# A state-space layer that starts from the unscaled sum, with 1/rms applied to its products and its decays masked by GpSimd

## The chip, the cores and the metric

The kernel runs on one core of a Trainium2 chip. The metric is the device time of one execution in microseconds (us). Below, PE is TensorE, DVE is VectorE, ACT is ScalarE, POOL is GpSimd and SP is the engine that issues most DMAs.

## The reference, cut to what matters

Two blocks run one after the other on 256 tokens of width 1024. The first ends with a mixture of 32 experts, whose weighted outputs are added to the stream. The second begins with a state-space layer that reads the normed stream:

```python
x = x + hier_moe(hn, ...)                      # x2 in the kernel
# second block, layer 0
u = x * rsqrt(mean(x*x) + EPS) * w             # rms_norm
proj = u @ in_w                                # z | x, B, C | dt
xbc = silu(conv4(proj[x, B, C]) + conv_b)      # 4 taps along the tokens, per channel
dt = softplus(proj[dt] + dt_bias);  a = dt * -exp(a_log)
a_cum = cumsum(a in chunks of 128 tokens)
decay_in = exp(where(causal, a_cum[t] - a_cum[s], -inf))     # per head, 32 heads
y = (C B^T * decay_in) x dt + state terms + D x
y = group_rms_norm(y * silu(z)) @ out_w
```

Afterwards come a second layer (latent attention) and a last norm, which the change doesn't touch.

## The kernel before, in words

Everything is in one program whose engines work through queues fixed when it is built; semaphores tie them together. Matmuls of weights at high accuracy are made of three products: a weight chunk `raw` is split into a high part by ACT (`W`, the cast in L101) and a low part by DVE (the subtraction in L101), both in a tile `whl`. Four to six such tiles exist.

Experts run in 8 groups of 4. For group q, `gate_up(q)` and `down(q)` multiply 32 rows by streamed weights; the side work `ex_side(q)` scatters the outputs of the group before back to the tokens (`scatter`: four products of the one-hot matrix `ST` with `ysb`, 128x512 each, L1096, added to `x2_sb` on DVE, L1097). After group 7's `down` its own scatter follows, each of its parts with a sum of squares on ACT (L352), then the check on whether an expert got more tokens than its rows hold (`overflow`, an If that all engines pass, L1663), then 1/rms (`rstd_of`).

The state-space layer turns `x2` with the diagonal `dr` of 1/rms (`norm_T`, 32 products of 128x128, L376). These pieces, times the gain, become `uh` and `ul` (ACT L379, DVE L380), the layer's input with features on partitions. Nine products into `acc` stand ahead of it (L1162). The units of the layer follow in this order: z0 (`gemm_first`, L411 to L413, 48 products of 512 columns, tokens on partitions), dt (24 small ones), then B0, B1, C0, C1, x0, x1, z1, x2, z2, x3, z3 (`fine_feat` and `fine_tok`, L417, 96 products of 256 columns or 48 of 512). Each fills one of two PSUM tiles `acc` of 128x1024. A queue of generators `Q` weaves other work between the products of a unit: `conv` on the unit just done, `decay(g)` for 8 groups of 4 heads, `silus`, `couple(g)` (C B^T times the decays `L`), `ssd(g)`, `gate` and so on.

`decay(g)` takes two heads at a time. Two products with the 64-row selector `id2` spread the cumulated decays over 128 partitions (L1233), 20 products of the unit later one product adds `negm`, minus 2 to the 100th where not causal (L1241), and ACT takes the exponentials, 128x128 each: two with bias `toend` (L1237), four with bias `ncum` (L1246). `conv` reads `acc` on ACT (four 128x256, L1255) and on DVE (twelve, L1260).

Of the kernel before, what the change touches and what calls it, by code (L numbers as in the profile page):

```python
# [18 lines left out]
P = 128  # L19
T = 256  # L20
# [10 lines left out]
WARM2 = 9  # L31
# [180 lines left out]
def model_kernel(ctx: ExitStack, tc: tile.TileContext, ap, out, taps=None, stop=None):  # L212
# [64 lines left out]
    def gain_row(pool, v):  # L277

        g = pool.tile([P, D], F32, name="gb", tag="gb")
        return g, nc.sync.dma_start(g, v.to_broadcast([P, D]))  # L280
# [104 lines left out]
    def gemm_first(xh, xl, norm, ps, steps):  # L385

        cs = {}
        for step in steps:  # L390
            if step is None:
                W.behind = ()
                continue
# [575 lines left out]
    with ExitStack() as b2:  # L969
# [105 lines left out]
        def down(q):  # L1075
            y = [yp.tile([P, 512], F32, name="yps") for _ in range(2)]
            h = hT.pop(q)
            for k in range(4):
                ws, used = W.whole(2)
                for half in range(2):  # L1080
                    for j in range(4):
                        nc.tensor.matmul(y[half][quad(j)], h[:, k, quad(j)], ws[j // 2][:, j % 2, HALF[half]],  # L1082
                                         start=(k == 0), stop=(k == 3))
                W.done(used)
            ys[q] = w2.tile([P, 1024], F32, name="ysb", bufs=1)
            for half in range(2):
                nc.scalar.copy(ys[q][:, HALF[half]], y[half])  # L1087

        def scatter(q, ST, done=None):

            y = ys.pop(q)
            for half in range(2):
                s = HALF[half]
                for t in range(2):
                    m = mp.tile([P, 512], F32, name="m")
                    nc.tensor.matmul(m, ST[:, t * P:(t + 1) * P], y[:, s], start=True, stop=True)  # L1096
                    nc.vector.tensor_add(x2_sb[:, t, s], (x2_sb if q else x_sb)[:, t, s], m)  # L1097
                    if done:
                        done(t, half)
                    yield  # L1100
# [13 lines left out]
        for q in range(8):  # L1114
            run_steps(gate_up(q), ex_side(q))
# [8 lines left out]
        idr = k2.tile([P, P], F32R, name="idr")  # L1124
        nc.vector.tensor_copy(idr, ident)
        id2 = k2.tile([64, 32], F32R, name="id2")
        nc.vector.tensor_add(id2, ident[:64, 0:32], ident[:64, 32:64])
        negm = k2.tile([P, P], F32R, name="negm")
        nc.vector.tensor_scalar(negm, G, -2.0 ** 100, None, op0=OP.mult)
# [3 lines left out]
        def x2_square(t, q):  # L1133
            square_sum(x2_sb[:, t, HALF[q]], junk, x2ss[:, t, q:q + 1])
# [16 lines left out]
    with ExitStack() as b3:  # L1151
# [11 lines left out]
        gemm_first(uh, ul, [norm_T(t, r2[t], R_N2, k3, mp, uh, ul) for t in range(2)], ps,  # L1163
                   ((None, 0), (None, 1), 0, 1, (None, 2), 0, 0, (None, 3), 0, 0, (0, 0), (0, 1), 1, 1, (0, 2), (0, 3),
                    1, 1, (1, 0), (1, 1), (1, 2), (1, 3)))
        zt = {0: w2.tile([P, 2, 512], F32, name="zs")}
        nc.scalar.activation(zt[0].rearrange("p a b -> p (a b)"), ps, AF.Silu)
# [3 lines left out]
        for k in range(8):  # L1171
            mm3(ps_d[:32, :T], h[:, k], l[:, k], uh[:, k], ul[:, k], k == 0, k == 7)
        nA = wk.tile([P, 32], F32, name="nA")
        xf = wk.tile([32, T], F32, name="xf")
        nc.scalar.activation(xf, ps_d[:32, :T], AF.Identity, bias=vec[:32, R_DTB:R_DTB + 1])
# [4 lines left out]
        chl = wk.tile([64, T], F32R, name="chl")  # L1180
# [26 lines left out]
        def sums():  # L1207
# [6 lines left out]
            nc.scalar.copy(chl, cum)  # L1214
# [12 lines left out]
        def decay(g):  # L1227

            for j in range(2):
                m = mp.tile([P, 2, T], F32, name="m")  # L1230
                for i in range(2):
                    h = 4 * g + 2 * j + i
                    nc.tensor.matmul(m[:, i], id2[:, h:h + 1].to_broadcast([64, P]), chl, start=(i == 0), stop=False,  # L1233
                                     skip_group_check=True)
                for i in range(2):
                    h = 4 * g + 2 * j + i
                    nc.scalar.activation(L[g][:, 1, 2 * j + i], m[:, i, P:], AF.Exp, bias=toend[:, h:h + 1])  # L1237
                for _ in range(10):
# [4 lines left out]
                for i in range(2):  # L1243
                    h = 4 * g + 2 * j + i
                    for c in range(2):
                        last["exp"] = nc.scalar.activation(L[g][:, 2 * c, 2 * j + i], m[:, i, c * P:(c + 1) * P],  # L1246
                                                           AF.Exp, bias=ncum[:, c, h:h + 1])
# [4 lines left out]
        def conv(ps, ct, f0):  # L1252
            for n in range(4):
                f = f0 + n
                nc.scalar.activation(ct[:, n], ps[:, n * T:(n + 1) * T], AF.Identity, bias=vcol(R_CB + f),  # L1255
                                     scale=convw[:, 3, f:f + 1])
            for k in range(2, -1, -1):
                d = 3 - k
                for n in range(4):
                    nc.vector.scalar_tensor_tensor(ct[:, n, d:], ps[:, n * T:(n + 1) * T - d],  # L1260
# [117 lines left out]
        for kind, u in (("x", 0), ("x", 1), ("z", 1), ("x", 2), ("z", 2), ("x", 3), ("z", 3)):  # L1378
# [7 lines left out]
            else:  # L1386
                Q.weave(fine_tok(uh, ul, ps), 48)
                zt[u] = w2.tile([P, 2, 512], F32, name="zs")
                z = nc.scalar.activation(zt[u].rearrange("p a b -> p (a b)"), ps, AF.Silu)  # L1389
# [30 lines left out]
    with ExitStack() as b4:  # L1420
# [6 lines left out]
        fw, dma = gain_row(k2, ap["final_norm_w_2"][None, :])  # L1427
# [230 lines left out]
def overflow(tc, nc, ap, raw, mp, yp, ep, ovi, wov, rx, g2, iof, ident, x_sb, x2_sb, after):  # L1658
# [4 lines left out]
    with tc.If(n > 0):  # L1663
        with ExitStack() as es:
            ov = es.enter_context(tc.tile_pool(name="ov", bufs=1))
            xf = raw.tile([P, 8, T], F32, name="raw", tag="raw")
            h4 = raw.tile([P, 4, 512], F32, name="raw", tag="raw")
# [11 lines left out]
            with tc.For_i(0, 32) as e:  # L1679
# [9 lines left out]
                def load(name, k0, n):  # L1689

                    wt = ov.tile([P, 1024], F32, name="owt")
# [6 lines left out]
                for name in ("w_expert_gate", "w_expert_up"):  # L1698
                    m = [ep.tile([P, 512], F32, name="ea") for _ in range(2)]
                    for k in range(8):  # L1700
                        if k % 2 == 0:
                            wt = load(name, k, 2)
                        for t in range(2):
                            nc.tensor.matmul(m[t], xf[:, k, t * P:(t + 1) * P], wt[:, k % 2], start=(k == 0),
# [6 lines left out]
                hT = ov.tile([P, 4, T], F32, name="ohT")  # L1711
# [5 lines left out]
                for half in range(2):  # L1717
                    s = slice(half * 512, half * 512 + 512)
                    y = [yp.tile([P, 512], F32, name="yps") for _ in range(2)]
                    for k in range(4):  # L1720
                        wt = load("w_expert_down", k, 1)
                        for t in range(2):
                            nc.tensor.matmul(y[t], hT[:, k, t * P:(t + 1) * P], wt[:, 0, s], start=(k == 0),
# [3 lines left out]
            for t in range(2):  # L1727
                for half in range(2):
                    after(t, half)
# [62 lines left out]
```

## Time and profile before

| | us |
|---|---|
| time, median of 3 runs (1091.69 to 1092.43) | 1092.33 |
| the profiled execution's own time | 1093.37 |
| its span | 1091.7 |
| mean granted TensorE clock in it | 0.992 |
| 240 to 635 us of the span | experts |
| 635 to 648.5 us | end of the experts to the state-space layer's first product |
| 648.5 to 877 us | state-space layer |

The profile was taken from one execution, 1.04 us longer than the median of the runs. Time in its rows is counted from the span's start. A stage is read by which engine is busy throughout, and by what an engine's idle time ended on.

### The profile page before, as it was taken

What the parts mean: (1) busy time and instruction counts of PE and PEld (TensorE: products, weight loads), DVE (VectorE), ACT (ScalarE), POOL (GpSimd) and SP (SyncE); (2) the same over time, 40 slices, a digit from 0 to 9 for tenths busy, and PEclk for the clock granted to TensorE, in tenths of its full rate; (3) what the DMA queues carried; (4) which work ended last, traced back from release to release, by engine and by line L of the source; (5) the groups of instructions that cost most, each with busy time, mean ns of one, the idle gap of its engine ahead of it and who ended that gap; (6) DMA issues with size and microseconds to landing.
All of it is one profiled execution on the core that took longest, in us unless ns stands there. A gap on an engine that the chain in (4) does not pass through costs nothing. (4 is left out here: it accounts for less than half of the span.)

```text
span 1091.7 us, 14807 instructions
## 1 busy us (share of the span) xinstructions
PE 977.3 (90%) x5981; PEld 687.9 (63%) x5981; DVE 492.1 (45%) x1085; ACT 393.7 (36%) x740; POOL 0.2 (0%) x4
## 2 busy tenths in 40 slices
PE   8999998998779696878866679999999999999997
PEld 6999986442314141322311149899998879999985
DVE  8687565121102020101001057589597576468763
ACT  5556542000000000000000046784855565476652
POOL 0000000000000000000000000000000000000000
PEclk9999998999999999999999999999999999999999
DMA  8444898999999999999999955444234446343331
GB/s 297 158 155 155 298 409 333 399 409 409 409 409 409 409 409 409 409 409 410 409 409 409 409 200 204 147 134 163 99 125 185 145 150 213 121 139 122 123 110 39
DMA packets 97096, 293.64 MB, mean 269 GB/s; under 512 B 6912, under 2 KB 12032, under 8 KB 97024
## 3 DMA queue, kind: packets, MB, share of 16 engines
q1 hardware_dynamic: 96736, 292.13, 71.3%
q8 instruction: 48, 0.79, 0.3%
q10 hardware_dynamic: 288, 0.52, 0.1%
q14 instruction: 24, 0.20, 0.0%
HBM read 291.58 MB, written 1.05 MB: 268 GB/s over the span
## 5 line engine op out<-in xcount | busy, mean ns | idle before, releaser
L101 DVE TENSOR_TENSOR whl<-raw,whl 128x1024 fp32r<-128x1024 f32 (+2 forms) x175 | 202.9, 1171 | 83.5 <-ACT whl L101 81.5
L101 ACT CAST whl<-raw 128x1024 fp32r<-128x1024 f32 (+2 forms) x175 | 175.4, 1012 | 130.1 <-PE acc L413 53.6
L1056 PE MATMUL ea<-raw,xg 128*32 128x512 f32 x1024 | 161.3, 605 | 54.0 <-DMA raw<-in_w_expert_up_dram 48.5
L1056 PEld LDWEIGHTS ea<-raw,xg 128*32 128x32 f32 x1024 | 33.4, 109 | 162.3 <-DMA raw<-in_w_expert_up_dram 93.2
L1082 PE MATMUL yps<-raw,hT 128*32 128x512 f32 x512 | 106.3, 598 | 32.1 <-DMA raw<-in_w_expert_down_dram 26.6
L417 PE MATMUL acc<-u,whl 128*128 128x256 f32 x768 | 103.2, 286 | 0.0
L417 PEld LDWEIGHTS acc<-u,whl 128*128 128x128 f32 x768 | 94.5, 189 | 2.4
L1082 PEld LDWEIGHTS yps<-raw,hT 128*32 128x32 f32 x512 | 22.4, 109 | 110.2 <-DMA raw<-in_w_expert_down_dram 64.8
L1097 DVE TENSOR_TENSOR x_sb<-x_sb,m 128x512 f32<-128x512 f32 x32 | 22.0, 688 | 148.2 <-PE m L1096 148.2
L1065 DVE TENSOR_TENSOR hx<-sg,ea 128x512 f32<-128x512 f32 x8 | 5.5, 689 | 170.9 <-PE ea L1056 170.9
L917 PEld LDWEIGHTS m<-Sr,x_sb 128*128 128x128 f32 x224 | 55.0, 334 | 8.8 <-issue 8.1
L1087 ACT COPY ysb<-yps 128x512 f32<-128x512 f32 x16 | 9.3, 586 | 129.7 <-PE yps L1082 129.7
L917 PE MATMUL m<-Sr,x_sb 128*128 128x128 f32 x224 | 55.8, 402 | 0.0
L411 PE MATMUL acc<-hh,whl 128*128 128x256 f32 x192 | 55.8, 290 | 0.0
L1073 ACT COPY hT<-m 128x512 f32<-128x512 f32 x8 | 4.7, 585 | 138.8 <-PE m L1071 138.8
L413 PE MATMUL acc<-hh,whl 128*128 128x256 f32 x192 | 54.7, 285 | 0.0
L412 PE MATMUL acc<-hl,whl 128*128 128x256 f32 x192 | 54.3, 283 | 0.0
L417 PE MATMUL bank<-whl,yhl 128*128 128x512 f32 x192 | 46.0, 395 | 0.4 <-ACT zs L1389 0.4
L1040 ACT COPY ST<-m 128x256 f32<-128x256 f32 x8 | 3.0, 373 | 108.6 <-PE m L1038 108.6
L417 PE MATMUL bank<-whl,oh 128*128 128x512 f32 x128 | 41.0, 398 | 0.0
L417 PEld LDWEIGHTS bank<-whl,yhl 128*128 128x128 f32 x192 | 35.7, 188 | 8.1 <-ACT zs L1389 0.6
L417 PE MATMUL acc<-whl,u 128*128 128x512 f32 x144 | 40.7, 410 | 0.0
(401 smaller groups left out, 1775.5 us busy)
## 6 DMA issues: line engine op xcount, KB each, us to landing
raw<-in_w_expert_gate_dram SPq DMA_DIRECT2D x64, 1024.0 KB, 18.4
raw<-in_w_expert_up_dram SPq DMA_DIRECT2D x64, 1024.0 KB, 18.5
raw<-in_w_expert_down_dram SPq DMA_DIRECT2D x64, 1024.0 KB, 18.4
raw<-in_ssm_in_w_dram SPq DMA_DIRECT2D x24, 1024.0 KB, 5.2
raw<-in_w_in_dram SPq DMA_DIRECT2D x15, 1024.0 KB, 5.3
raw<-in_mla_in_w_dram SPq DMA_DIRECT2D x10, 1024.0 KB, 5.2
raw<-in_ssm_out_w_dram SPq DMA_DIRECT2D x8, 1024.0 KB, 5.2
raw<-in_mla_out_w_dram SPq DMA_DIRECT2D x8, 1024.0 KB, 5.0
```

The costliest lines, as they stand in the source:

```text
L101: pair = self.last = (nc.scalar.copy(hv, v), nc.vector.tensor_sub(lv, v, hv.bitcast(F32)))
L411: nc.tensor.matmul(o, ah, bh, start=first, stop=False, skip_group_check=True)
L412: nc.tensor.matmul(o, ah, bl, start=False, stop=False, skip_group_check=True)
L413: nc.tensor.matmul(o, al, bh, start=False, stop=last, skip_group_check=True)
L417: nc.tensor.matmul(o, a, b, start=first and i == 0, stop=last and i == 2, skip_group_check=True)
L917: nc.tensor.matmul(m[:, k], x_sb[:, t, half * 4 + k::8], Sr[q][:, t], start=(t == 0), stop=(t == 1))
L1056: nc.tensor.matmul(ps[quad(j)], x[:, k, quad(j)], ws[j // 2][:, j % 2, kk * 512:kk * 512 + 512], start=(k == 0), stop=(k == 7))
L1065: nc.vector.tensor_mul(hx[q], sg, ps)
L1073: nc.scalar.copy(hT[q].rearrange("p a b -> p (a b)"), m)
L1082: nc.tensor.matmul(y[half][quad(j)], h[:, k, quad(j)], ws[j // 2][:, j % 2, HALF[half]], start=(k == 0), stop=(k == 3))
L1087: nc.scalar.copy(ys[q][:, HALF[half]], y[half])
L1097: nc.vector.tensor_add(x2_sb[:, t, s], (x2_sb if q else x_sb)[:, t, s], m)
```

## The change

Three things are altered.

The overflow check stands ahead of group 7's `gate_up` instead of behind its scatter. Its body, which isn't entered unless an expert is over its rows, takes its tiles from the ring of expert weights.

The state-space layer starts from the sum without 1/rms. Before group 7's `down`, 16 products with `ident` turn `x2` of groups 0 to 6 into four PSUM tiles `xT` (L1137); after `down`, eight products of `y7` with `ST7`, 128x256, add group 7 to them (L1142). ACT and DVE form `uh` and `ul` from `xT` with the gain alone (L1170, L1171). The scatter of group 7 itself, its squares, and 1/rms by 13 small DVE operations come inside z0 (`x2_rows`, L1181). 1/rms, `r2`, is then applied to what comes out: as the scale of the silu of z (two 128x512 instead of one 128x1024), as a row tile `R2` (from two products of `ones` with a diagonal `dr`, L1214) for dt, and in `conv` by one DVE product 128x1024 from `acc` into an SBUF tile `cv` (L1301), which ACT and DVE then read instead of `acc`. `WARM2`'s nine products go.

The decays: `id2` and `chl` are padded from 64 to 128 rows (L1279); the `negm` products are gone; DVE adds `ncum` to the PSUM tile and writes `L` (16 times 128x512, L1285); GpSimd sets what isn't causal to -1e30 (8 `affine_select` of 128x1024, L1292); ACT takes one exponential of 128x1024 per group (L1294) in place of eight.

```diff
         for q in range(8):
+            if q == 7:
+                overflow(tc, nc, ap, ring, mp, yp, ea, ovi, wov, rx, g2, iof, ident, x_sb, x2_sb)
             run_steps(gate_up(q), ex_side(q))
...
+        xT = [ea.tile([P, 2, T], F32, name="ea") for _ in range(4)]
+        for k in range(8):
+            for t in range(2):
+                nc.tensor.matmul(xT[k // 2][:, k % 2, t * P:(t + 1) * P], x2_sb[:, t, k * P:(k + 1) * P], ident,
+                                 start=(k % 2 == 0 and t == 0), stop=False, skip_group_check=True)
         down(7)
+        y7 = ys.pop(7)
+        for k in range(8):
+            nc.tensor.matmul(xT[k // 2][:, k % 2], y7[:, k * P:(k + 1) * P], ST7, start=False, stop=True,
+                             skip_group_check=True)
         W.stop = None
-        W.ahead(2)
-        for _ in scatter(7, rows[7], x2_square):
-            pass
         b2i.close()
-        overflow(tc, nc, ap, raw2, mp, yp, ea, ovi, wov, rx, g2, iof, ident, x_sb, x2_sb, x2_square)
...
-        r2 = [rstd_of(x2ss[:, t]) for t in range(2)]
         ps = acc()
-        for _ in range(WARM2):
-            nc.tensor.matmul(ps[:, :512], idr, negm[:, None, :].to_broadcast([P, 4, P]), start=True, stop=True)
-        gemm_first(uh, ul, [norm_T(t, r2[t], R_N2, k3, mp, uh, ul) for t in range(2)], ps,
...
+                for k in range(k0, k0 + 4):
+                    m = xT[k // 2][:, k % 2]
+                    nc.scalar.activation(uh[:, k], m, AF.Copy, scale=vcol(R_N2 + k))
+                    nc.vector.scalar_tensor_tensor(ul[:, k], m, vcol(R_N2 + k), uh[:, k].bitcast(F32),
+                                                   op0=OP.mult, op1=OP.subtract)
...
+                    nc.tensor.matmul(m, ST7[:, t * P:(t + 1) * P], y7[:, HALF[i]], start=True, stop=True)
+                    nc.vector.tensor_add(x_sb[:, t, HALF[i]], x_sb[:, t, HALF[i]], m)
+                    square_sum(x_sb[:, t, HALF[i]], junk, x2ss[:, t, i:i + 1])
...
+        gemm_first(uh, ul, None, ps,
+                   ((None, 0), u_parts(0), (None, 1), u_parts(4), (0, 0), (1, 0), (None, 2), (0, 1), (1, 1), x2_rows,
+                    (None, 3), lambda: x2_rest[0](), (0, 2), (1, 2), (0, 3), (1, 3)))
+        dr = [k3.tile([P, P], F32, name="dr", bufs=2) for _ in range(2)]
...
+                i = nc.scalar.activation(z[:, t], ps[:, t * 512:t * 512 + 512], AF.Silu, scale=r2[:, t:t + 1])
...
+            nc.tensor.matmul(m[:, t * P:(t + 1) * P], ones, dr[t], start=True, stop=True)
+        nc.scalar.copy(R2, m[:, :T])
...
+                nc.vector.tensor_tensor(L[g][:, 0::2, 2 * j:2 * j + 2], m.rearrange("p i (c t) -> p c i t", c=2),
+                                        ncum[:, :, h:h + 2, None].to_broadcast([P, 2, 2, P]), op=OP.add)
...
-                nc.tensor.matmul(m.rearrange("p i t -> p (i t)"), idr, negm[:, None, :].to_broadcast([P, 4, P]),
-                                 start=False, stop=True, skip_group_check=True)
...
+            v = L[g][:, 0::2]
+            nc.gpsimd.affine_select(v, v, pattern=[[0, 2], [0, 4], [1, P]], compare_op=OP.is_ge, fill=NEG, base=0,
+                                    channel_multiplier=-1)
+            last["exp"] = nc.scalar.activation(v, v, AF.Exp)
...
+            cv = k2.tile([P, 4, T], F32, name="cv", tag="ysb")
+            nc.vector.tensor_mul(cv, ps.rearrange("p (n t) -> p n t", n=4), R2[:, None, :].to_broadcast([P, 4, T]))
```

On PE, at the entry of the state-space layer, the queue of before ends so, behind group 7's scatter (the branches are those of the If):

```order
L1679 COMPARE_AND_BRANCH
L1679 UNCONDITIONAL_BRANCH
L1663 UNCONDITIONAL_BRANCH x2
L1162 MATMUL acc<-negm,idr 128x512 x9
L376 MATMUL m<-dr,x_sb 128x128 x8
L411 MATMUL acc<-whl,u 128x512
L412 MATMUL acc<-whl,u 128x512
```

and that of the change this, where `ea` are the tiles `xT`:

```order
L1137 MATMUL ea<-cst,x_sb 128x128 x4
L1073 MATMUL m<-cst,hx 128x128 x4
L1137 MATMUL ea<-cst,x_sb 128x128 x12
L1084 MATMUL yps<-raw,hT 32x512 x32
L1142 MATMUL ea<-ST_3805,ysb 128x256 x8
L413 MATMUL acc<-whl,u 128x512
L414 MATMUL acc<-whl,u 128x512
```

Between the last expert product and the first of the layer there are eight products now; scatter, If, the nine and the first turns are out of that place.

On PE in the middle of the decays, pairs of heads among the products of B0 and B1 stood like this before:

```order
L1241 MATMUL m<-negm,idr 128x512
L1233 MATMUL m<-chl,id_3645 128x256 x2
L417 MATMUL acc<-u,whl 128x256 x20
L1241 MATMUL m<-negm,idr 128x512
L417 MATMUL acc<-u,whl 128x256 x36
```

and pairs now stand like this:

```order
L1279 MATMUL m<-chl,id_3801 128x256 x2
L419 MATMUL acc<-u,whl 128x256 x20
L1279 MATMUL m<-chl,id_3801 128x256 x2
L419 MATMUL acc<-u,whl 128x256 x56
L1279 MATMUL m<-chl,id_3801 128x256 x2
```

The mask product is gone from each pair, and the selector products have 128 rows.

On DVE, in the stretch of the decays and of the convolution of C1, before:

```order
L101 TENSOR_TENSOR whl<-raw,whl 128x1024 x4
L1260 SCALAR_TENSOR_TENSOR CT<-acc,vec,CT 128x255 x4
L1260 SCALAR_TENSOR_TENSOR CT<-acc,vec,CT 128x254 x4
L1260 SCALAR_TENSOR_TENSOR CT<-acc,vec,CT 128x253 x4
L101 TENSOR_TENSOR whl<-raw,whl 128x1024
L1279 TENSOR_TENSOR L<-L,m 128x1536
L101 TENSOR_TENSOR whl<-raw,whl 128x1024 x2
```

and of the change (`m` is a decay's PSUM tile, `acc` that of a unit):

```order
L100 TENSOR_TENSOR whl<-raw,whl 128x1024
L1285 TENSOR_TENSOR L<-m,ncum 128x2x256
L1301 TENSOR_TENSOR cv<-acc,R_3898 128x1024
L100 TENSOR_TENSOR whl<-raw,whl 128x1024 x2
L1309 SCALAR_TENSOR_TENSOR CT<-cv,vec,CT 128x255 x4
L1309 SCALAR_TENSOR_TENSOR CT<-cv,vec,CT 128x254 x4
L1309 SCALAR_TENSOR_TENSOR CT<-cv,vec,CT 128x253 x4
L1328 TENSOR_TENSOR L<-L,m 128x1536 x2
L100 TENSOR_TENSOR whl<-raw,whl 128x1024 x2
```

The additions of the decays and the product into `cv` stand between the weights' low parts (L101 before, L100 now), and the twelve steps of the convolution read `cv` instead of `acc`.

## Rows read from the trace of the kernel before

**Rows 1.** Stretches: busy PE, PEld, DVE, ACT, POOL (x instructions), granted clock, DMA share, GB/s.

```profile
240.00:635.00 395.00, 303.55 (x1524) 99.84 (x1516) 35.12 (x73) 17.61 (x33) 0.00 (x0) 1.00 1.03 409
635.00:648.50 13.50, 9.83 (x36) 5.95 (x33) 9.62 (x33) 7.41 (x16) 0.00 (x0) 0.87 0.43 137
...
682.00:730.00 48.00, 47.92 (x354) 43.31 (x354) 30.77 (x53) 40.02 (x99) 0.00 (x0) 1.00 0.40 132
730.00:754.00 24.00, 24.00 (x191) 23.30 (x190) 23.68 (x32) 14.29 (x20) 0.00 (x0) 1.00 0.54 176
754.00:842.00 88.00, 87.65 (x583) 78.83 (x582) 70.12 (x129) 56.85 (x112) 0.00 (x0) 1.00 0.39 133
```

**Rows 2.** Timeline, 630 to 684 us: start, duration, instruction, idle time before it.

```profile
635.49 3.95 PE L1096 MATMUL m<-ysb,ST 128*128 128x512 f32 x8
...
642.27 0.63 ACT L352 ACTIVATE junk<-x_sb 128x512 f32<-128x512 f32 x1
...
643.10 3.91 PE L1162 MATMUL acc<-negm,idr 128*128 128x512 f32 x9 [3.66 <-ACTq L1663]
...
648.55 0.48 PE L411 MATMUL acc<-whl,u 128*128 128x512 f32 x1
```

**Rows 3.** Chain that ended last, 630 to 744 us: start, duration, what.

```profile
647.01 1.78 PE m L376 x16
...
651.32 0.23 PE acc L413
651.55 0.89 PE m L376 x8
...
664.34 3.58 PE acc L417 x30
...
676.12 0.24 DVE hr L1198
```

**Rows 4.** The same chain, 690 to 700 us, one pair of heads.

```profile
693.41 0.23 PE m L1241
693.64 0.43 PE m L1233 x2
694.07 2.48 PE acc L417 x20
```

**Rows 5.** Groups on DVE, 664 to 842 us: count, busy us, mean ns, idle before.

```profile
L101 DVE TENSOR_TENSOR whl<-raw,whl 128x1024 fp32r<-128x1024 f32 x48 | 57.2, 1218 | 8.1 <-ACT whl L101 7.9
...
L1298 DVE TENSOR_TENSOR y<-m,row 128x512 f32<-128x512 f32 x8 | 5.4, 679 | 0.0
```

**Rows 6.** Tile `kt`: a DVE product of 128x1024 from PSUM, ns.

```profile
L578 DVE TENSOR_TENSOR kt<-acc,ny x1: 1225/1225/1225, 32.7 to 32.7; 128x1024 f32<-128x1024 f32 x1
```

**Rows 7.** Waits of DVE, 683 to 729 us: total, times, longest.

```profile
DVE CT L1260 <- ACT CT L1255: 7.2, 2, 3.9
DVE whl L101 <- ACT whl L101: 5.1, 3, 2.7
DVE BT L1260 <- ACT BT L1255: 4.8, 1, 4.8
```

**Rows 8.** Timeline of DVE, 664 to 735 us, the end of C1's convolution.

```profile
723.95 4.76 DVE L1260 SCALAR_TENSOR_TENSOR CT<-acc,vec,CT 128x255 f32<-128x255 f32 x12 [3.24 <-ACT CT L1255]
```

**Rows 9.** Waits of PE, 635 to 880 us: total, times, longest.

```profile
PE bank L417 <- ACT zs L1389: 0.4, 1, 0.4
PE m L1210 <- DVE aa L1203: 0.3, 1, 0.3
```

**Rows 10.** Groups on ACT, 648 to 842 us.

```profile
L1246 ACT ACTIVATE L<-m,ncum 128x128 f32<-128x128 f32 x64 | 18.2, 378 | 6.3 <-PE m L1241 6.3
...
L1266 ACT ACTIVATE xc<-xc 128x1024 f32<-128x1024 f32 x4 | 4.2, 1061 | 0.0
```

**Rows 11.** Groups on POOL, whole span (one of four alike).

```profile
L1781 POOL MEMSET const-float32-1.0<- 128x1 f32 x1 | 0.1, 99 | 0.0
```

**Rows 12.** DMA issues: count, KB each, median us from issue to landing.

```profile
raw<-in_w_expert_down_dram SPq DMA_DIRECT2D x64, 1024.0 KB, 18.4
```

More of the change, by code (lines that the diff above doesn't have):

```diff
@@ L30 @@
 WARM = 10
-WARM2 = 9
 WARM3 = 2
@@ L275, in model_kernel, with gain_row @@
     nc.sync.dma_start(x_sb[:, 0], ap["x"][0, 0:P, :])
-    def gain_row(pool, v):
-        g = pool.tile([P, D], F32, name="gb", tag="gb")
+    def gain_row(pool, v, tag="gb"):
+        g = pool.tile([P, D], F32, name="gb", tag=tag)
         return g, nc.sync.dma_start(g, v.to_broadcast([P, D]))
@@ L392, in gemm_first @@
                 W.behind = ()
+                continue
+            if callable(step):
+                step()
                 continue
@@ L1084, in down, with scatter @@
                 W.done(used)
-            ys[q] = w2.tile([P, 1024], F32, name="ysb", bufs=1)
+            ys[q] = (w2 if q < 7 else k2).tile([P, 1024], F32, name="ysb", bufs=1)
             for half in range(2):
-                nc.scalar.copy(ys[q][:, HALF[half]], y[half])
-        def scatter(q, ST, done=None):
+                (nc.vector.tensor_copy if half and q == 7 else nc.scalar.copy)(ys[q][:, HALF[half]], y[half])
+        def scatter(q, ST):
             y = ys.pop(q)
@@ new lines, in x2_rows, with rest @@
+        def x2_rows():
+            x2ss = wk.tile([P, 2, 2], F32, name="x2ss")
+            for t in range(2):
+                for i in range(2):
+                    m = mp.tile([P, 512], F32, name="m")
+                    nc.tensor.matmul(m, ST7[:, t * P:(t + 1) * P], y7[:, HALF[i]], start=True, stop=True)
+                    nc.vector.tensor_add(x_sb[:, t, HALF[i]], x_sb[:, t, HALF[i]], m)
+                    square_sum(x_sb[:, t, HALF[i]], junk, x2ss[:, t, i:i + 1])
+            def rest():
+                v = small.tile([P, 16], F32, name="qv")
+                nc.vector.tensor_add(v[:, :2], x2ss[:, :, 0], x2ss[:, :, 1])
+                nc.vector.tensor_scalar(v[:, :2], v[:, :2], 1.0 / D, EPS, op0=OP.mult, op1=OP.add)
+                nc.vector.tensor_copy(r2, rsqrt_newton(v[:, :2], 2))
+            x2_rest.append(rest)
@@ new lines, in model_kernel, with z_silu @@
+        x2_rest = []
+        gemm_first(uh, ul, None, ps,
+                   ((None, 0), u_parts(0), (None, 1), u_parts(4), (0, 0), (1, 0), (None, 2), (0, 1), (1, 1), x2_rows,
+                    (None, 3), lambda: x2_rest[0](), (0, 2), (1, 2), (0, 3), (1, 3)))
+        dr = [k3.tile([P, P], F32, name="dr", bufs=2) for _ in range(2)]
+        for t in range(2):
+            nc.vector.tensor_scalar(dr[t], ident, r2[:, t:t + 1], None, op0=OP.mult)
+        def z_silu(z, ps):
+            for t in range(2):
+                i = nc.scalar.activation(z[:, t], ps[:, t * 512:t * 512 + 512], AF.Silu, scale=r2[:, t:t + 1])
+            return i
@@ L1172, in model_kernel @@
             mm3(ps_d[:32, :T], h[:, k], l[:, k], uh[:, k], ul[:, k], k == 0, k == 7)
+        m = mp.tile([P, 512], F32, name="m")
+        for t in range(2):
+            nc.tensor.matmul(m[:, t * P:(t + 1) * P], ones, dr[t], start=True, stop=True)
+        nc.scalar.copy(R2, m[:, :T])
         nA = wk.tile([P, 32], F32, name="nA")
         xf = wk.tile([32, T], F32, name="xf")
-        nc.scalar.activation(xf, ps_d[:32, :T], AF.Identity, bias=vec[:32, R_DTB:R_DTB + 1])
+        nc.vector.tensor_mul(xf, ps_d[:32, :T], R2[:32])
+        nc.scalar.activation(xf, xf, AF.Identity, bias=vec[:32, R_DTB:R_DTB + 1])
         xd, ab, en, zz, z2, hr, dt = (wk.tile([P, 2, 32], F32, name=n)
@@ L1179, in model_kernel @@
         cum = wk.tile([64, T], F32, name="cum")
-        chl = wk.tile([64, T], F32R, name="chl")
+        chl = wk.tile([P, T], F32R, name="chl")
+        nc.vector.tensor_scalar(chl[64:P, 0:P], ident[64:P], 0.0, None, op0=OP.mult)
+        nc.vector.tensor_scalar(chl[64:P, P:T], ident[64:P], 0.0, None, op0=OP.mult)
         ncum = wk.tile([P, 2, 32], F32, name="ncum")
@@ L1426, in model_kernel @@
         uh, ul = u[:, 0], u[:, 1]
-        fw, dma = gain_row(k2, ap["final_norm_w_2"][None, :])
+        fw, dma = gain_row(k2, ap["final_norm_w_2"][None, :], "ysb")
         order(tc, dma, W.dma)
@@ L1655, in model_kernel, with overflow @@
         tap("x4", x_sb)
-def overflow(tc, nc, ap, raw, mp, yp, ep, ovi, wov, rx, g2, iof, ident, x_sb, x2_sb, after):
+def overflow(tc, nc, ap, ring, mp, yp, ep, ovi, wov, rx, g2, iof, ident, x_sb, x2_sb):
     E = mybir.EngineType
@@ L1726, in overflow @@
                         nc.vector.tensor_add(x2_sb[:, t, s], x2_sb[:, t, s], y[t])
-            for t in range(2):
-                for half in range(2):
-                    after(t, half)
 R_CW, R_CB, R_NW, R_QN, R_KVN, R_PS, R_SUB, R_Q, R_K = 0, 128, 160, 176, 179, 181, 185, 186, 187
```

55 lines of the change are left out of this document (24 added, 31 removed).

## The prediction

> **What bounds the kernel now.** I read the table of stretches first [rows 1]: per stretch it shows which engine is busy all the time. In the experts, 240 to 635 us, PE works 303.55 of 395 us while the DMA share is 1.03 at 409 GB/s, so transfers set that stage and PE has about a fifth of it to spare. From 635 to 648.5 us neither PE nor DMA is full, and the granted clock is 0.87: this is the entry into the state-space layer. In the layer PE is busy 47.92 of 48 us from 682 to 730, 24 of 24 after, 87.65 of 88 after that. So there a product removed from PE is time, as long as nothing else is late. DVE is the one to watch: 30.77 of 48, then 23.68 of 24, then 70.12 of 88.
>
> The timeline of the entry came next [rows 2]. The last expert products end about 635.5; the scatter's four take 3.95 us; then PE stands 3.66 us, released by ACT at the If, which ACT reaches only after its squares (the last begins at 642.27); nine products take 3.91 us to 647.0; the layer's first product is at 648.55. The chain that ended last [rows 3] runs through these, through 16 turning products (1.78 us) and, inside z0, through 16 more (two lots of 0.89 us). Last I read the chain over one pair of heads [rows 4]: mask 0.23, selectors 0.43, 20 products of the unit 2.48, together 3.14 us.
>
> **The entry: about 5 us.** Between the last expert product and the first of the layer there remain eight products 128x256, as many columns as the scatter's four, so at most 3.95 us [rows 2]. They begin with the second half of `ysb` at about 635.6, so the layer begins at 639.5 instead of 648.55: 9.0 us earlier. That holds if `uh` and `ul` follow each turned tile; ACT and DVE have nothing else there than the first weights. The 16 turns that go ahead of `down(7)` cost 1.78 us at the price of [rows 3] in a stage where PE waits for transfers, hidden; without that cover they would cost that. PE has no long idle there any more, so the low clock should go too: 512 columns took 3.91/9 = 0.43 us in the nine products against 0.23 in z0 [rows 2, 3].
>
> Inside z0, 2 x 0.89 = 1.78 us of turns go and four scatter products come, at most 3.95. z0 and dt therefore end 9.0 - 2.2 = 6.8 us earlier, dt at 664.34 - 6.8 = 657.5.
>
> Now 1/rms, which nothing waited for inside the layer before. The four products stand behind 25 of z0's: 639.5 + 25 x 0.23 + 3.95 = 649.2. An addition (0.68) and a weight's low part queued ahead of it (1.22) [rows 5] make 651.1, a square of 0.63 [rows 2] 651.7. The 13 small operations follow each other on DVE at 0.24 like `hr` [rows 3], with three more low parts of 1.22 between them: 3.1 + 3.7 = 6.8, so r2 is there at 658.5. The diagonals, their products and the silu of z, which frees the `acc` tile that B0 wants, take 0.5 to 1.2 more: B0 begins at about 659.3 instead of 664.34, a gain of 5.0. On PE all of B0 is queued behind the wait for `dr`. Bounds: 6.8 if r2 comes in time, 3 if another low part or two falls ahead of it. I take 5.0.
>
> **The decays on PE: 8.3 us.** Per pair of heads 3.14 us become 20 products and two full-row selectors of 256 columns at 3.58/30 = 0.119 us [rows 3]: 22 x 0.119 = 2.62. That is 0.52 less, 16 times: 8.3 us. Both terms together are 13.3.
>
> **What is given back: about 5.3 us.** DVE gets 16 additions of 512 columns from PSUM at 0.68 [rows 5], and 8 products into `cv`, at 1.225 like the one of `kt` [rows 6]. The convolution's steps I leave at their price; reading SBUF instead of PSUM may make them a little shorter or longer. Of these, 12 additions and three `cv` fall into 682 to 730: 8.2 + 3.7 = 11.9. DVE's waits in that stretch, all for ACT, sum to 7.2 + 5.1 + 4.8 = 17.1 us [rows 7], so the sum fits. But PE now wants to be through sooner, by 5.0 + 12 x 0.52 = 11.2 us at the first couplings. DVE's work up to the end of C1's convolution, at 723.95 + 4.76 = 728.7 [rows 8], is 30.77 - 1.2 + 11.9 = 41.5 us; begun at 677 it ends at 718.5 without any wait, 10.2 earlier. So it limits the gain by 1.0 with no idle at all, and each of the three convolutions still has `cv` and a first pass of ACT ahead of it. I take 2.0 (bounds 1.0 and 4).
>
> From 730 to 754 DVE is full already and gets two `cv`, 2.45 us. PE's waits on DVE from 635 to 880 us are one of 0.3 us for `aa`, ahead of this stretch [rows 9], so how far behind it may fall isn't seen: half of it, 1.1 (bounds 0 and 2.45). From 754 to 842 it has 17.9 us idle for four additions and two `cv`, 5.2: nothing.
>
> At the layer's end PE waits 0.4 us, for the last z on ACT [rows 9], so the chain from x3's convolution to the gate has no cover to spare; it gets a `cv`, 1.2, and whatever DVE is behind. I take 2.2 (bounds 0.8 and 4).
>
> ACT loses 7 of 8 exponentials per group, 8 x 0.378 - 1.06 = 2.0 us [rows 10]. They stand in its queue behind POOL now, and behind each of them weight casts that PE wants. ACT has 8 us idle in 682 to 730 and six of these groups, so over 3 us of room per group: a select of S us costs nothing by this path while S is below about 3. The trace has no select; POOL shows only 128x1 fills of 0.1 us [rows 11]. The nearest passes over 1,024 elements are ACT's 1.06 and DVE's 1.22. I take S near 1.2 to 2, with no upper bound known.
>
> **The overflow check: nothing.** SP passes it between the loads of group 7's up and down weights. A chunk is issued 18.4 us before it lands [rows 12], so a stop of a few us on SP or PE is absorbed by what is queued; a stop beyond that would cost one for one.
>
> **Sum.** -5.0 - 8.3 + 2.0 + 1.1 + 2.2 = -8.0 us: 1085.4 on the profiled execution's 1093.37, which stands 1.04 above the median, so 1084.3 against the median of 1092.33.
>
> **The rivals.** *DVE and POOL in each other's way: slower.* The convolution's steps read two SBUF tiles now, as the weights' low parts always did. If such an operation stands while a select runs, each select puts its S on DVE, in a stretch that DVE bounds. Of its 42.7 us there, some 12 low parts (14.6) and three convolutions (14.3) are of this kind, 68%. Six selects fall there: 6 x 0.68 x S = 4.1 S. It decides at S of about 2 us (8.2 against 8.0); at S = 3 the kernel takes 1084.3 + 12.2 = 1096.5. Against it: DVE's other operations read PSUM. Nothing in the trace has POOL and DVE at work together, so it stays open. The Trainium skill has this as a rule (SBUF — State Buffer, Who interferes with whom): a DVE instruction with two SBUF inputs contends with a GpSimd instruction that reads SBUF; of DVE's two-port modes it says that whichever comes second is fully blocked. No trace here shows it. The Trainium skill (GPSIMD Engine Reference, 3.1 Elementwise — side-by-side cycle accounting) gives 769 ns for 512 elements in a tight loop; an estimate from that page is 1.5 us for a select, by which this rival's sum would be 1090.6.
>
> *The whole gain.* The waits on DVE don't come because PE's woven queue finds other work: -13.3 + 1 = about 1080. For it: PE's waits on DVE were one of 0.3 us [rows 9]. Against it: DVE was full in 730 to 754.
>
> *The gain runs into new waits.* r2 two us later, DVE's three terms at their upper bounds: -3 - 8.3 + 4 + 2.45 + 4 = about -1, 1091.5. For it: r2's 13 operations sit behind weights that ACT delivers late whenever PE frees a tile late.
>
> *The check stops the stream of expert weights*, so that the change doesn't do what it says: more than 18 us of stop needed; a few chances in a hundred, time 1095.
>
> **How the numbers follow.** The forecast, gains of 4.5 to 11 (1081 to 1088), 0.40; the whole gain, 0.17; new waits, 0.18, of which 0.11 is within 0.2% (2.2 us, about what a measurement of this kernel can tell from no change) and 0.07 faster; slower by POOL, 0.22, or by the check, 0.03. Faster 0.64, same 0.11, slower 0.25. The range reaches from just under the whole gain, 1077.5, to the POOL rival at S of 3, 1097; what is left out is S above that and an entry without any wait for r2. Faster and slower both hold weight, so the forecast's own range is 1081 to 1088.
>
> **What the next profile shows.** The entry: first product of the layer near 639.5, the clock at 1.00 there, and a wait of 1 to 3 us on PE for `dr` or the `acc` tile behind dt. The decays: no mask product, pairs 2.6 us apart. Given back: PE waits at the first couplings, DVE near full from 677 to 745, and waits of PE at the layer's end. POOL: the length of a select, and whether DVE's low parts of 1.22 us become longer beside one. The forecast is wrong if selects take over 2 us and stretch DVE, if r2 comes after 662, or if PE waits for transfers in group 7.

## The result, and the profile after

The changed kernel takes 1078.7 us (median of 4 runs, 1078.46 to 1080.9) against 1092.38 (4 runs, 1091.69 to 1092.97): ratio 0.988, 95% interval 0.9862 to 0.9897, or 13.7 us less by the medians. The profiled execution took 1080.9, its span is 1079.2, 12.5 us less than the span of before. The forecast of 1084.3 had the direction: 8.0 us less were forecast, 13.7 measured. The time lies inside the wide range of 1077.5 to 1097, but 2.3 us below the 1081 to 1088 that the forecast kept for itself with a chance of 0.40. It is nearest to the rival "the whole gain" (about 1080, chance 0.17).

The stretches of the layer after, to be held against [rows 1] (busy us of PE, PEld, DVE, ACT, POOL, then granted clock, DMA share, GB/s):

```profile
636.00:645.00 9.00, 8.87 (x39) 7.22 (x40) 7.53 (x14) 7.14 (x14) 0.00 (x0) 1.00 0.41 117
...
677.00:690.00 13.00, 13.00 (x113) 13.00 (x112) 12.69 (x19) 10.49 (x22) 5.14 (x3) 1.00 0.36 122
690.00:718.00 28.00, 28.00 (x241) 28.00 (x240) 27.44 (x46) 21.30 (x36) 4.21 (x3) 1.00 0.53 167
718.00:730.00 12.00, 10.89 (x90) 10.53 (x90) 11.58 (x16) 9.91 (x13) 0.00 (x0) 1.00 0.37 127
```

DVE is as full as feared, 40.1 of 41 us from 677 to 718, and PE is full all the same. The clock of the entry is 1.00 where it was 0.87.

The timeline of the entry, against [rows 2] (the profile counts a product of two f32 operands in two passes, so x16 are eight products):

```profile
636.13 3.69 PE L1142 MATMUL ea<-ST,ysb 128*128 128x256 f32 x16 [0.73 <-ACT ysb L1089]
...
639.47 0.58 PE L413 MATMUL acc<-whl,u 128*128 128x512 f32 x1
...
645.67 3.60 PE L1181 MATMUL m<-ysb,ST 128*128 128x512 f32 x8
```

and PE's next one, between dt and B0:

```profile
657.01 0.28 PE L415 MATMUL acc<-u,whl 128*32 128x256 f32 x1
658.00 0.71 PE L1214 MATMUL m<-dr,one 128*128 128x128 f32 x4 [0.71 <-DVE dr L1198]
658.98 3.84 PE L419 MATMUL acc<-u,whl 128*128 128x256 f32 x30 [0.27 <-ACT zs L1202]
```

The layer begins at 639.47 (9.1 us earlier), dt ends at 657.1 (7.2 earlier), B0 begins at 658.98 (5.4 earlier than 664.34): the third is what the late 1/rms leaves of the second. Counted in both timelines from the end of the last expert product, B0 begins after 28.6 us before and 23.6 now, 5.0 us earlier.

PE's waits from 600 to 880 us, the rows that belong to the layer, against [rows 9]:

```profile
PE bank L419 <- ACT zs L1202: 1.3, 1, 1.3
...
PE m L1325 <- ACT CT L1315: 1.1, 1, 1.1
...
PE m L1214 <- DVE dr L1198: 0.7, 1, 0.7
PE m L1342 <- ACT xc L1315: 0.4, 1, 0.4
PE acc L419 <- ACT zs L1202: 0.3, 1, 0.3
PE m L1342 <- DVE L L1328: 0.2, 1, 0.2
```

Behind B0, PE waits 1.1 + 0.4 + 0.2 us around the couplings and 1.3 at the out product, in sum 3.0 where it was 0.7.

POOL's timeline, and DVE's in the same stretch:

```profile
681.34 2.02 POOL L1292 TENSOR_SCALAR_AFFINE_SELECT L<-L 128x1024 f32<-128x1024 f32 x1 [680.76 <-DVE L L1285]
685.11 2.02 POOL L1292 TENSOR_SCALAR_AFFINE_SELECT L<-L 128x1024 f32<-128x1024 f32 x1 [1.75 <-DVE L L1285]
687.44 1.10 POOL L1292 TENSOR_SCALAR_AFFINE_SELECT L<-L 128x1024 f32<-128x1024 f32 x1 [0.31 <-DVE L L1285]
```

```profile
681.19 1.22 DVE L100 TENSOR_TENSOR whl<-raw,whl 128x1024 fp32r<-128x1024 f32 x1
682.32 0.69 DVE L1285 TENSOR_TENSOR L<-m,ncum 128x512 f32<-128x512 f32 x1
682.92 1.52 DVE L100 TENSOR_TENSOR whl<-raw,whl 128x1024 fp32r<-128x1024 f32 x1
...
687.29 1.21 DVE L1301 TENSOR_TENSOR cv<-acc,R 128x1024 f32<-128x1024 f32 x1
```

A select takes 1.10 us beside the product into `cv`, which reads PSUM and one SBUF tile. Begun at 681.34, while a low part with two SBUF inputs runs from 681.19, it ends only at 683.36, about 1.0 us after the low part is done; and the low part that begins at 682.92, inside the select, takes 1.52 instead of 1.22 and ends 1.1 us after the select. So whichever of the two begins second waits for the other: both ends lie within 0.15 us of what a full wait gives.

### The profile page after: what moved, and what is told of

The parts are those of the page before. It is cut to its first block, busy times and chain, and to the rows that moved or that the text cites. A ratio compares the mean times of both kernels' runs of the same rounds, so it can differ in the third digit from the quotient of the medians.

```text
span 1079.2 us, 14781 instructions
## 1 busy us (share of the span) xinstructions
PE 969.7 (90%) x5976; PEld 684.2 (63%) x5976; DVE 510.6 (47%) x1100; ACT 382.4 (35%) x678; POOL 13.0 (1%) x12
## 5 line engine op out<-in xcount | busy, mean ns | idle before, releaser
L100 DVE TENSOR_TENSOR whl<-raw,whl 128x1024 fp32r<-128x1024 f32 (+2 forms) x175 | 204.7, 1175 | 80.5 <-ACT whl L100 78.8
L100 ACT CAST whl<-raw 128x1024 fp32r<-128x1024 f32 (+2 forms) x175 | 175.5, 1009 | 142.0 <-PE acc L415 53.6
L1058 PE MATMUL ea<-raw,xg 128*32 128x512 f32 x1024 | 165.5, 634 | 48.3 <-DMA raw<-in_w_expert_up_dram 43.3
L1084 PE MATMUL yps<-raw,hT 128*32 128x512 f32 x512 | 103.6, 610 | 32.1 <-DMA raw<-in_w_expert_down_dram 27.3
L419 PE MATMUL acc<-u,whl 128*128 128x256 f32 x768 | 97.5, 282 | 0.3 <-ACT zs L1202 0.3
L1099 DVE TENSOR_TENSOR x_sb<-x_sb,m 128x512 f32<-128x512 f32 x28 | 19.3, 688 | 163.5 <-PE m L1098 163.5
L907 DVE TENSOR_TENSOR xg<-m,vec 128x512 f32<-128x512 f32 x14 | 9.7, 692 | 61.7 <-PE m L919 61.7
```

Source lines behind the costliest of these rows:

```text
L100: pair = self.last = (nc.scalar.copy(hv, v), nc.vector.tensor_sub(lv, v, hv.bitcast(F32)))
L419: nc.tensor.matmul(o, a, b, start=first and i == 0, stop=last and i == 2, skip_group_check=True)
L1058: nc.tensor.matmul(ps[quad(j)], x[:, k, quad(j)], ws[j // 2][:, j % 2, kk * 512:kk * 512 + 512], start=(k == 0), stop=(k == 7))
```

## The experiments

Executions differ by up to 3 us in when the experts end, so beside each ratio to the kernel before (95% interval) stand two times of the profiled execution: from the last expert product's end to the layer's first product, and from there to the first product of the layer's out matmul (`bank`).

| kernel | ratio | interval | entry us | layer us | both |
|---|---|---|---|---|---|
| before | 1 | | 13.0 | 182.4 | 195.4 |
| changed | 0.988 | 0.9862 to 0.9897 | 4.1 | 179.0 | 183.0 |
| changed, again | 0.9895 | 0.9879 to 0.9911 | 4.1 | 179.1 | 183.2 |
| turn alone | 0.9964 | 0.9951 to 0.9976 | 4.3 | 186.6 | 190.9 |
| decays alone | 0.9911 | 0.9896 to 0.9925 | 13.0 | 172.6 | 185.6 |
| full rows alone | 0.994 | 0.9926 to 0.9955 | 13.0 | 176.7 | 189.7 |
| check moved alone | 0.9993 | 0.9983 to 1.0003 | 12.1 | 182.7 | 194.8 |
| additions twice | 0.9896 | 0.9881 to 0.9911 | 4.1 | 178.3 | 182.4 |
| select thrice | 1.0019 | 1.0008 to 1.003 | 4.1 | 190.1 | 194.2 |
| 1/rms first | 0.9885 | 0.987 to 0.9901 | 4.1 | 177.5 | 181.5 |
| turns uncovered | 0.9906 | 0.9891 to 0.9921 | 6.9 | 177.6 | 184.5 |
| no select | 0.9876 | 0.986 to 0.9892 | 4.1 | 176.8 | 180.9 |
| select twice | 0.9952 | 0.9938 to 0.9967 | 4.1 | 184.4 | 188.5 |
| 1/rms first, couple later | 0.9879 | 0.9864 to 0.9895 | 4.1 | 176.9 | 181.0 |

**The turn alone.** The changed kernel with `decay` of before.

```diff
-            v = L[g][:, 0::2]
-            nc.gpsimd.affine_select(v, v, ...)
-            last["exp"] = nc.scalar.activation(v, v, AF.Exp)
+                nc.tensor.matmul(m.rearrange("p i t -> p (i t)"), idr, negm[:, None, :].to_broadcast([P, 4, P]), ...)
+                        last["exp"] = nc.scalar.activation(L[g][:, 2 * c, 2 * j + i], m[:, i, c * P:(c + 1) * P],
+                                                           AF.Exp, bias=ncum[:, c, h:h + 1])
```

> The changed kernel with the decays of before (64-row selectors, mask products on PE, exponentials of 128x128 with a bias; one small tile is shared to make room). Theory A, two savings of PE time that add up: the entry brought B0 forward by 5.4 us in the trace of the changed kernel and DVE has 17 us of waits left in the decays' stretch, so 5 us less than before, about 1087.4. Rival B, the entry's gain needs the lighter decays to live: cv's 9.8 us of DVE work and the late 1/rms eat it, 0 to 2 us less than before.

It takes 3.9 us less (2.6 to 5.3), both stretches together 4.5. Theory A in kind, a little under its number. The layer itself is 4.2 us longer than before: z0 holds 1.8 us more of products (3.60 for 2 x 0.89), 1/rms keeps B0 some 1.9 us behind dt's end, and PE's wait at the out product is 1.4 us where it was 0.4. These make 4.7; against them stands PE's wait of 0.3 us for `aa`, which is gone.

**The decays alone.** The kernel before with the three edits of `decay`.

```diff
-        id2 = k2.tile([64, 32], F32R, name="id2")
+        id2 = k2.tile([P, 32], F32R, name="id2")
-                nc.tensor.matmul(m.rearrange("p i t -> p (i t)"), idr, negm...)
+                nc.vector.tensor_tensor(L[g][:, 0::2, 2 * j:2 * j + 2], ..., ncum..., op=OP.add)
+            nc.gpsimd.affine_select(v, v, ...)
```

> The kernel before with the three edits of the decays alone (128-row selectors, DVE additions, GpSimd select with one exponential per group). Theory A: PE loses 8.3 to 9 us of products and DVE's 17 us of waits hide the 12 additions, so 8 us less than before, about 1084.4; together with the run of the turn alone the two sum to the whole change's 13.7. Rival B: part of the decays' gain runs into waits for DVE at the first couplings, 4 to 6 us less, and the rest of the 13.7 comes from the two together.

9.7 us less (8.2 to 11.3), 9.8 in the trace. Theory A, and more than its 8. With the turn alone it makes 13.6 us by the ratios, about the whole change. In the traces 4.5 + 9.8 = 14.3 against 12.4 together: 1.9 us are lost by having both, which the times don't resolve, and the 1.7 us of waits around the couplings stand in neither of the two alone. This kernel's layer has 0.3 us of waiting for `aa` and, as its last wait:

```profile
PE bank L417 <- ACT zs L1392: 0.2, 1, 0.2
```

**Full rows alone.** The kernel before with 128-row selectors, masks kept.

```diff
-        chl = wk.tile([64, T], F32R, name="chl")
+        chl = wk.tile([P, T], F32R, name="chl")
-                    nc.tensor.matmul(m[:, i], id2[:, h:h + 1].to_broadcast([64, P]), chl, ...)
+                    nc.tensor.matmul(m[:, i], id2[:, h:h + 1].to_broadcast([P, P]), chl, ...)
```

> The kernel before with only id2 and chl padded from 64 to 128 rows; the mask products stay. Theory A, the 64-row products cost more than their columns: a pair of selectors takes 0.43 us in the chain of before against 2 x 0.119 at full rows, 16 times 0.19, 3.0 us less than before. Rival B, the time is the mask's and the rows don't matter: 0 to 0.5 us less.

6.5 us less (4.9 to 8.1), 5.7 in the trace, about twice theory A. The chain over a pair of heads, against [rows 4]:

```profile
691.01 0.23 PE m L1243
691.24 0.24 PE m L1235 x2
691.48 2.35 PE acc L417 x20
```

The selectors go from 0.43 to 0.24, and the 20 products behind them, which the edit doesn't touch, from 2.48 to 2.35. In the kernel before, the layer's first two pairs stood together, and in the next ones the mask stood between two selectors:

```profile
681.55 0.66 PE m L1233 x4
...
682.76 0.31 PE m L1233
683.07 0.43 PE m L1241
```

A 256-column selector there took 0.31 instead of 0.12 and the mask 0.43 instead of 0.23. Four selectors in a row took 0.66 where two take 0.43, so each further one costs 0.12, no more than at full rows. So a change between 64 and 128 rows costs PE at the change, on whichever product comes next, some 0.1 to 0.2 us: my price by the selectors' own rows saw half of it. The Trainium skill (TensorEngine Tiling (Array Packing), Key Properties) says that changing the tiling mode drains TensorE. A price at each change agrees with that, if products of 64 and of 128 rows are two modes; that it is a drain, no run here shows.

**The check alone.**

```diff
+            if q == 7:
+                overflow(tc, nc, ap, ring, mp, yp, ea, ovi, wov, rx, g2, iof, ident, x_sb, x2_sb)
             run_steps(gate_up(q), ex_side(q))
...
-        overflow(tc, nc, ap, raw2, ..., x2_square)
```

> The kernel before with only the overflow check moved ahead of group 7. Theory A: PE's 3.66 us at the If were a wait for ACT's squares, which 1/rms needs anyway; the nine products move forward but the turn still waits for 1/rms, which DVE begins after the last square at 643.0; so within 1 us of before. Rival B, the If itself was the wait: up to 3.7 us less. Rival C, the check now stops the stream of expert weights: slower, by what the stop is over 18 us.

Ratio 0.9993 (0.9983 to 1.0003): no change that can be told, theory A. PE's wait is still there, and it ends on the addition now:

```profile
641.78 3.46 PE L1163 MATMUL acc<-negm,idr 128*128 128x512 f32 x9 [2.79 <-DVE x_sb L1097]
```

The 3.66 us that ended at the If were never the If's price; what the entry waited for was 1/rms. The trace's entry is 0.9 us shorter (12.1 against 13.0); in the times that doesn't show. And the experts' weights keep flowing: from 590 to 650 us PE waits 13.8 us for them, 14.6 before.

**The additions twice.**

```diff
+                nc.vector.tensor_tensor(junk..., m..., ncum..., op=OP.add)
                 nc.vector.tensor_tensor(L[g][:, 0::2, 2 * j:2 * j + 2], ...
```

> The changed kernel with each of the decays' 16 DVE additions made twice, the first time into a scratch tile that nobody reads. Theory A, DVE is full from 677 to 718 (40.1 of 41 us) and sets the first couplings: twelve more operations of 0.68 us ahead of them go into the time almost one for one, 6 to 9 us more than the changed kernel, about 1086. Rival B, PE's woven queue gives way and finds other products: under 3 us more.

Ratio 0.9896: theory A fell. 10.9 us more of DVE work, 8.2 of them where DVE is full, cost nothing that can be told (layer 178.3 against 179.0). PE's timeline shows why, in the order the program was built with. The products of the units between the last selectors and the first coupling, in the kernel before, in the changed one and in this one:

```profile
720.42 2.55 PE L417 MATMUL acc<-u,whl 128*128 128x256 f32 x20
...
723.04 6.13 PE L417 MATMUL acc<-u,whl 128*128 128x256 f32 x50
```

```profile
707.74 11.55 PE L419 MATMUL acc<-u,whl 128*128 128x256 f32 x97
```

```profile
707.45 18.74 PE L419 MATMUL acc<-u,whl 128*128 128x256 f32 x158
726.26 0.70 PE L1328 MATMUL m<-CT,BT 128*128 128x256 f32 x2
```

Before it is 70, 20 ahead of the last mask and 50 behind it; then 97 and 158. The places in the queue `Q` are the same in all three. With more DVE work the builder, which orders the engines' queues when the program is built, puts more of x0's products ahead of the coupling, and PE meets no wait there; its next wait, for x0's silu, is 1.4 us where it was 0.4. That DVE is full says nothing of the time here while PE has such work left.

**The select thrice, twice, and not at all.**

```diff
-            nc.gpsimd.affine_select(v, v, ...)
+            for _ in range(3):
+                nc.gpsimd.affine_select(v, v, ...)
```

Twice is `range(2)`. Without any, the kernel leaves the mask out:

```diff
-            nc.gpsimd.affine_select(v, v, ...)
-            last["exp"] = nc.scalar.activation(v, v, AF.Exp)
+            last["exp"] = nc.scalar.activation(v, v, AF.Exp, scale=0.0)
```

> The changed kernel with each select made three times on the same tile (the second and third change nothing), so that S is 3 x 1.1 = 3.3 us. Theory A, POOL and DVE exclude each other where DVE reads two SBUF tiles, and whichever begins later waits: each of 12 more selects ahead of the first couplings can hold a DVE operation for up to 1.1 us, and each is itself held; with DVE full there, 4 to 9 us more than the changed kernel, and selects of 1.1 and of 2 us side by side. Rival B, no exclusion, only ACT's queue behind POOL, which has over 3 us of room per group: 0 to 1 us more.

> The changed kernel with each select made twice (S = 2.2 us; the second changes nothing), the order on PE unchanged. Three times gave 11 us more in the trace. Theory A, a threshold: PE's order leaves the first coupling about no slack, so each us by which the chain add, select, exponential, silu ends later is a wait there; six selects each 1.1 us longer, part of it beside ACT's idle time, 3 to 6 us more than the changed kernel. Rival B, the cost begins only past 2.2 us: within 1 us of it.

> The changed kernel without GpSimd's selects, the exponential taken of zero times its argument: what isn't causal isn't masked, and all decays within a chunk become 1. The builder puts the first coupling behind 85 of the unit's products instead of 97. Theory A, at 1.1 us a select costs little, since the order on PE finds other products: PE's 1.1 us for the silu of C at the first coupling goes or halves, 0 to 1.5 us less than the changed kernel. Rival B, the select's exclusion with DVE and the exponentials behind it cost more than PE's wait shows: 3 us or more less.

The layer takes 176.8, 179.0, 184.4 and 190.1 us with no, one, two and three selects. None is 1.4 us less than one by the medians on one chip (1078.62 and 1080.04; the ratios' intervals overlap), theory A, and 2.2 less in the trace, between the theories. Two cost 5.4 more in the trace, theory A; by the ratios 6.2 to 7.9. Three cost 11.1, beyond theory A's 9; by the ratios 13.5 to 15.2; the profiled execution was 3.7 us shorter than the median of its runs. And it isn't the wait that theory A for three had in mind, that of full DVE: here the builder left 97 products ahead of the coupling, and the chain behind POOL comes out as a wait of PE. The first row is with two, the second with three:

```profile
723.04 1.21 PE L1326 MATMUL m<-CT,BT 128*128 128x256 f32 x2 [4.49 <-ACT CT L1316]
```

```profile
727.22 1.22 PE L1326 MATMUL m<-CT,BT 128*128 128x256 f32 x2 [9.77 <-ACT CT L1316]
```

The wait is not the whole price. Behind it the granted clock is 0.51 from 723 to 726 us with two selects, nearly the lower of the clock's two levels (1.2 of 2.4 GHz), where it is 1.00 in the changed kernel (719 to 722): the first coupling's first product takes 1.21 us instead of 0.70.

In the changed kernel that chain already sets the coupling. This is its chain over 700 to 722 us:

```profile
709.11 2.01 POOL L L1292
...
712.87 1.10 POOL L L1292
713.97 0.02 issue
714.00 1.06 ACT L L1294
715.06 1.97 ACT CT L1304 x4
...
717.04 1.28 ACT L1315
...
718.34 1.06 ACT BT L1315
719.40 0.95 ACT CT L1315
...
720.39 0.70 PE m L1325 x2
```

Two selects, an exponential, C1's first pass, the table load, two silus, the coupling: the last pair's mask is in it, ahead of a convolution that doesn't need it, because ACT works its queue in order. How much of the chain is the selects' own length and how much their being held up by DVE isn't separated: over all eight a select averages 1.60 us, 0.5 above an undisturbed one. With three selects DVE suffers as well. Twelve steps of a convolution, 4.8 us in the changed kernel, partly beside selects:

```profile
704.26 6.48 DVE L1310 SCALAR_TENSOR_TENSOR CT<-cv,vec,CT 128x255 f32<-128x255 f32 x12
```

**1/rms first.** The diagonals are made right behind r2, and later weights' low parts are ordered behind the second of them (`x2_rest[-1]`).

```diff
+            W.ahead(3)
+            W.behind = (None, x2_rest[-1])
         W.ahead()
```

> The changed kernel with 1/rms and its diagonals ahead of the low parts of later weights on DVE (three low parts of 1.22 us stood between its 13 operations). Theory A, the last wait of the entry is that of PE for the diagonals and the silu, about 1.0 + 0.6 us between dt's end at 657.1 and B0 at 659.0: it goes, 1 to 1.7 us less than the changed kernel. Rival B, the low parts that are put off are missed by B0, or the DVE-bound stretch behind gives it back: no change, or more.

B0 begins without a wait, 1.6 us earlier:

```profile
657.36 2.88 PE L422 MATMUL acc<-u,whl 128*128 128x256 f32 x22
```

In the trace the layer is 1.5 us shorter, theory A; the ratio, 0.9885, can't be told from the changed kernel's.

**The turns uncovered.** The 16 turns are ordered behind the last expert product.

```diff
+                order(tc, i, last_down[-1])
```

> The changed kernel with the 16 turning products put behind the last expert product instead of among group 7's waits for weights. Theory A, they cost nothing only because PE waits for transfers there: their 32 passes at 0.118 us, 3.6 to 3.8 us, less the wait of 0.7 us for ysb that they fill: 3 us more than the changed kernel. Rival B, ACT and DVE set the entry, not PE: under 1 us more.

```profile
634.06 3.84 PE L1140 MATMUL ea<-cst,x_sb 128*128 128x128 f32 x32
```

They take 3.84 us and the layer begins 2.8 us later, as theory A has it; by the out matmul 1.5 us of it are left, between the theories, since the gap ahead of B0 is 1.5 us shorter then. The ratio, 0.9906, is 1 to 3 us above the changed kernel's, with overlapping intervals. So PE sets the entry, and the turns are hidden where they are: the experts end at 635.4 with them and at 635.6 before.

**Both repairs.** 1/rms first, and the first coupling behind 108 products.

```diff
-                        (4.01, silus([...])), (4.21, couple(0)),
-                        (4.51, couple(1)), ...
+                        (4.01, silus([...])), (5.00, couple(0)),
+                        (5.00, couple(1)), ...
```

> The changed kernel itself, on the same chip as the next run, since runs of two chips differ by about as much as what is sought: 1078 to 1081, 1.1 to 1.3% less than before.

> The changed kernel with two repairs: 1/rms ahead of the low parts of later weights on DVE, as run before, and the first coupling behind 108 products instead of 97. Theory A: B0 begins 1.5 us earlier and PE's 1.1 us at the first coupling goes, 2 to 2.5 us less than the changed kernel run beside it. Rival B, later waits (x0's silu, the last z) take the gain back: under 1 us less.

On one chip 1078.77 us against 1080.04 for the changed kernel again (ratios 0.9879 and 0.9895, with overlapping intervals). In the trace 181.0 against 183.2: the wait at the first coupling is gone, but x0's silu makes PE wait 0.8 + 0.4 us next. 2.2 us less in the trace is theory A, 1.3 in the times lies between the theories: not resolved.

## Why the prediction was right or wrong

**The entry, 5 us: right, in part by luck.** First product forecast at 639.5, measured 639.47; dt's end 657.5, measured 657.1; r2 at 658.5, measured 657.6; B0 at 659.3, measured 658.98. The wait was the one named, PE for `dr` and the `acc` tile. But errors cancelled. The eight products began 0.5 us later than forecast, after a wait for `ysb` that I didn't have, and took 3.34 instead of 3.95. r2 came 0.9 earlier, as its 13 steps follow each other at 0.20 and not 0.24, and from r2 to B0 it took 1.4 us where I had 0.8. One number was half of what it is: I priced the 16 turns at 1.78 us from a row whose x16 are eight products in two passes (the 32 records of L376 are 16 products); uncovered they take 3.84. It didn't matter, because they are covered.

**The decays, 8.3 us: right in kind, mis-sized by 1.5.** Alone they give 9.8 in the trace. The pair in [rows 4] was the cheapest kind; pairs with the mask between the selectors paid 64-to-128-row changes more often.

**Given back, 5.3 us: this is the step that failed.** Gross gains of 5.4 and 9.8 make 15.2; the two stretches of the trace became 12.4 shorter, so 2.8 came back: 1.0 at the out product (forecast 2.2) and 1.7 around the couplings (forecast 2.0 + 1.1). The 2.0 and 1.1 were worked out from DVE's busy time against the moment at which PE "wants to be through", as if PE's queue were fixed. The moment itself was forecast well: the first coupling begins at 720.39 instead of 729.25, 8.9 us earlier, and I had 11.2 less 2.0. What was wrong is that the difference would be idle time of PE. The additions run twice show that it isn't: the builder puts 70, 97 or 158 products ahead of the coupling, and full DVE cost nothing there. What in DVE's work moves the builder wasn't isolated; two or three selects in place of one left it at 97. This is the mechanism of the rival "the whole gain", which I gave 0.17; that its time comes out so close is partly luck, since its gains and its waits were both about 2 us too small. The wait that did come, 1.1 us, ends on ACT and is the chain behind POOL, not DVE's work; without selects it is gone.

**POOL: the rival's mechanism is there, its price and its threshold were off.** I put the select's whole length on DVE where both read SBUF, which gave 4.1 S, or 4.5 us at S = 1.1, and a turning point at S near 2. The rows show that it is shared: whoever is second waits, three selects of six took 2.02 and only two low parts lengthened, by 0.3. So of my signs of being wrong one came in the letter, selects over 2 us that stretch DVE, and it cost little: leaving the selects out saves 1.4 to 2.2 us. What grows with S is the chain through ACT: layer times of +5.4 us for one more select and +11.1 for two more, about 5 us per us of S from the second select on. My estimate that ACT had 3 us of room per group before a select costs anything is refuted: the second already costs. The threshold at which the whole change would be lost lies near three selects (ratio 1.0019), S = 3.3, not 2.

The rule of the Trainium skill named ahead (SBUF — State Buffer, Who interferes with whom) agrees with the rows: 2.02 beside a low part of two SBUF inputs, 1.10 beside a product from PSUM. The estimate of 1.5 us from the Trainium skill (GPSIMD Engine Reference, 3.1 Elementwise — side-by-side cycle accounting) was above the 1.10 of an undisturbed select here.

**The check, nothing: right**, ratio 0.9993.

What stays open is how much of the difference between 12.5 us (the spans) and 13.7 (the medians) is the experts' stage, whose end moves by up to 3 us from execution to execution.

## What to carry to other kernels

When work is woven between an engine's products by a builder, an engine that becomes full isn't yet a price: look up, in the order of the changed program, how many products now stand ahead of the consumer, and price only what that cover can't hide. What the cover didn't hide here is a chain that an in-order engine forms: a result that nobody needs soon (the last mask) delays everything queued behind its consumer on ACT. With 11 more products ahead of the coupling that wait was gone too, and the next one grew. And before a mask or a sum is taken off PE, look at row counts: padding a 64-row product to 128 rows gave more than half of the decays' gain by itself.

## What the runs showed of the hardware

- A GpSimd select of 128x1024 f32 took 1.10 us alone, and 2.02 when it began inside a 1.22 us DVE subtraction of two SBUF tiles; a subtraction that began inside a select took 1.52. A DVE product with one SBUF input beside a select kept its length (1.21), and so did the select.
- Products next to one of another row count took 0.31 instead of 0.12 us (256 columns) and 0.43 instead of 0.23 (512 columns); twenty products behind a 64-row one took 2.48 instead of 2.35.
- After PE had stood 4.49 us, its granted clock was 0.51 over the next 3 us, and a product of 128x256 in two passes took 1.21 instead of 0.70.
- 10.9 us of added DVE work, 8.2 of it where DVE was full, left the kernel's time where it was.
